# A decoder layer's output projection by seven half-block products over chunk pairs, moved to the end

## The chip, the cores and the metric

One core of one Trainium2 chip runs one launch of the kernel. The metric is device time in microseconds (us). A core has a matmul engine (PE, with its weight loads PEld), a vector engine (DVE), an activation engine (ACT), a third engine for elementwise work (POOL), and SP, which here only issues transfers. Each engine runs its own instructions in order and waits on semaphores for the others. SBUF is the memory on the core, PSUM the banks into which PE accumulates, DRAM the memory off the core.

## What is computed

One layer on 2048 tokens of width 1024, all float32:

- `h = RMSNorm(x) * (1 + scale) + shift`, with shift, scale and gate from a vector `c`
- `P = h @ W_in`, seven groups of 512 columns
- four gMLP groups (`u * mixed(LN(v)) * silu(gate)` in chunks of 128 tokens) and four retention heads (GroupNorm, times `silu(gate)`) give `y`, 2048 x 1024
- `out = x + gate * RMSNorm_post(y @ W_out)`

The change is about the last line's product `y @ W_out`, 2048 x 1024 by 1024 x 1024, and about what is done beside it.

## The kernel before

**Arithmetic.** A float32 operand is split into a high part that PE takes exactly and a low part that is the rest. A block product is three matmuls, high x high, high x low, low x high (`mm3`, `z_mms`), each of 128 rows by up to 512 columns. A high part is a copy on ACT, a low part a subtraction on DVE (`split`, line 170).

**Stages.** The tokens are worked in two halves of 1024, eight chunks of 128 each, two quads of four chunks. A half goes through: retention values (`prv`), queries and keys of two pairs of heads (`pqk`), gMLP values (`pv`), each by `token_unit`, eight slots per chunk; then six *units* (`unit`, line 650), which make the gates and u as seven products of half blocks in place of eight (a scheme of Winograd's kind: blocks A11 to A22 of h and their sums S1 to S4, blocks B11 to B22 of the weights and their sums T1 to T4, three banks X, Y, Z). A unit is 7 products x 4 blocks x 3 = 84 matmuls. Each product's result, after additions out of PSUM on DVE (`then`, `add`), multiplies a tile of y (`used`); in a half's last unit DVE does that for two of the products (`quick`), otherwise POOL does. Then comes the *projection*: `out_unit` per chunk, 16 blocks of w_out x 3 matmuls into two banks, and `out_tail`, which squares (ACT), takes the root (POOL), scales by `gg` (the row gate x g_post), adds x (DVE) and stores. The last chunk of all has its own code (`out_last`).

**What sets the order.** Instructions are issued in the order of the program text on each engine. `Slots` is a clock in that text: a slot is one block (three matmuls), `slots.tick()` moves on, `slots.at(n, fn)` puts `fn`'s instructions n slots later. So each engine has a fixed order, and the engines are tied together only by waits.

**Weights.** `pump` takes the next block of a list (`worder`) and splits it (`wsplit`), and issues transfers for up to three blocks ahead (`wdma`). In the units one product's first slot pumps one block; a half's last unit pumps more (`LAST_PUMPS`). In a unit four weight sums are made by POOL (`combine`). w_out is loaded and split once in each half, 16 blocks, under the last unit and the first `out_unit`.

**Beside the units.** `gate_row` (line 914), started with the first half's second unit, makes `gg`: in four rounds of 33 slots eight additions of 256 columns on DVE over weights that SP loads into three rotating buffers, then a spread over the partitions by two matmuls. `xdiag2` and `xrow` make a row of the second half's 1/rms by matmul, and `hbuild` makes the second half's h, 16 blocks, under the first half's projection, two per chunk; half of them start on POOL and half on DVE.

**Memory.** `slot` takes one of 80 buffers of 2 KB per partition (`big`); all blocks, parts and h live there. y is two tiles per part and half (`yR` for retention, `yT` for gMLP), in pools that are opened and closed as a stack (`opened`, `closed`).

## Time and profile before

| | us |
|---|---|
| median of 3 runs | 895.89 (895.77 to 896.27) |
| the profiled execution | 896.12 |
| its span, first to last instruction | 894.3 |
| PE busy | 865.1 |
| DVE busy | 607.3 |
| POOL busy | 323.8 |
| ACT busy | 294.0 |

The mean granted clock of PE is 0.997 of full. In the rows below a line's number is that of the kernel above; `x240` is a count. In rows of windows the columns are: the stretch, its length, then for PE, PEld, DVE, ACT and POOL the busy time and instructions that began there, the granted clock of PE, the share of the DMA engines and GB/s. A timeline's row may merge several instructions of one kind. What stands in brackets is the idle time of the engine before the instruction and what ended it. PE's matmuls overlap, so their durations are longer than the distance of their starts.

### The profile page before, as it was taken

The page shows a single profiled execution, that of the slowest core. Times are in us where ns is not written, and L with a number is a line of the kernel's source. Part 1 is how long each engine was busy: PE and PEld are TensorE (multiplying, and loading weights), DVE is VectorE, ACT ScalarE, POOL GpSimd, SP SyncE. Part 2 cuts the span into 40 slices and gives each one's busy share as a digit, 9 for nine tenths or more (in the row PEclk, how much of TensorE's full clock was granted, in tenths as well). Part 3 has the DMA queues.
Part 4 walks back from the last instruction along what each step waited for, and adds up shares of the span by engine and source line. Part 5 has one row for each costly group of instructions (what it writes and reads, how often), then busy time and mean ns, then how long its engine had stood idle before and what let it go on. Part 6 is the DMA issues. An engine that isn't in the chain of part 4 may idle for free.

```text
span 894.3 us, 11921 instructions
## 1 busy us (share of the span) xinstructions
PE 865.1 (97%) x4198; PEld 717.4 (80%) x4198; DVE 607.3 (68%) x1217; ACT 294.0 (33%) x585; POOL 323.8 (36%) x399
## 2 busy tenths in 40 slices
PE   2999999999999999899999999999999999999997
PEld 1778888888888878678888888888888888888886
DVE  4989876666997887976676755566499644475332
ACT  4673223233363422533351012012126432352221
POOL 2040353345755654111110033333378554620000
PEclk9999999999999999999999999999999999999999
DMA  8971232210012323744453200110001112142222
GB/s 325 331 246 35 95 107 71 84 35 19 1 48 93 105 94 104 259 153 147 148 177 106 82 1 24 60 36 1 1 1 48 48 57 84 38 143 107 104 94 83
DMA packets 43835, 84.86 MB, mean 95 GB/s; under 512 B 5248, under 2 KB 10496, under 8 KB 43776
## 3 DMA queue, kind: packets, MB, share of 16 engines
q1 hardware_dynamic: 43776, 84.10, 27.6%
q8 instruction: 33, 0.54, 0.3%
q14 instruction: 26, 0.21, 0.1%
HBM read 75.69 MB, written 8.39 MB: 94 GB/s over the span
## 4 chain that ended last, share of the span: by engine, by line
PE 86%; DVE 5%; DMA 4%; issue 3%; ACT 1%; SPq 1%; POOL 0%; DVEq 0%; POOLq 0%; ACTq 0%
PE z L969 6%; PE z L968 6%; PE z L967 6%; PE pqk L210 6%; PE pqk L208 6%; PE pqk L209 6%; PE pv L208 3%; PE pv L210 3%; PE pv L209 3%; PE pY L210 3%; PE pY L209 3%; PE pY L208 3%; PE prv L210 2%; PE prv L209 2%; PE prv L208 2%
## 5 line engine op out<-in xcount | busy, mean ns | idle before, releaser
L208 PE MATMUL pqk<-wh,hh 128*128 128x512 f32 x240 | 102.4, 427 | 0.0
L968 PE MATMUL z<-wl,yh 128*128 128x512 f32 (+1 forms) x264 | 101.1, 383 | 0.2 <-DVE wl L176 0.2
L969 PE MATMUL z<-wh,yl 128*128 128x512 f32 (+1 forms) x264 | 101.1, 383 | 0.0
L967 PE MATMUL z<-wh,yh 128*128 128x512 f32 (+1 forms) x264 | 101.1, 383 | 0.0
L210 PE MATMUL pqk<-wh,hl 128*128 128x512 f32 x240 | 94.5, 394 | 0.0
L209 PE MATMUL pqk<-wl,hh 128*128 128x512 f32 x240 | 93.7, 390 | 0.0
L471 POOL TENSOR_TENSOR rA<-rA,rB 128x512 f32<-128x512 f32 x32 | 42.5, 1327 | 134.8 <-DVE rB L463 100.8
L176 DVE TENSOR_TENSOR wl<-wr,wh 128x512 fp32r<-128x512 f32 x94 | 83.9, 915 | 5.8 <-ACT wh L173 5.8
L485 ACT COPY qkT<-tp 128x512 f32<-128x512 f32 x32 | 18.8, 587 | 172.7 <-PE tp L476 172.7
L579 DVE SCALAR_TENSOR_TENSOR zo<-z,zrs,gg 128x512 f32<-128x512 f32 x30 | 22.4, 745 | 59.2 <-POOL zrs L574 59.2
L173 ACT CAST wh<-wr 128x512 fp32r<-128x512 f32 x96 | 55.5, 619 | 19.9 <-DMA wr<-in_win 7.7
L573 POOL TENSOR_SCALAR zrs<-zss 128x1 f32<-128x1 f32 x15 | 4.5, 300 | 149.0 <-ACT jz L570 149.0
L968 PEld LDWEIGHTS z<-wl,yh 128*128 128x128 f32 x264 | 49.6, 188 | 10.2 <-DVE wl L176 0.5
L969 PEld LDWEIGHTS z<-wh,yl 128*128 128x128 f32 x264 | 49.6, 188 | 10.0 <-DVE yl L559 0.4
L967 PEld LDWEIGHTS z<-wh,yh 128*128 128x128 f32 x264 | 49.6, 188 | 9.8 <-ACT wh L173 0.2
L210 PEld LDWEIGHTS pqk<-wh,hl 128*128 128x128 f32 x240 | 45.0, 188 | 10.4
L637 POOL TENSOR_TENSOR yT<-yT,c 128x512 f32<-128x512 f32 x20 | 30.3, 1516 | 61.3 <-DVE c L658 40.1
L208 PE MATMUL pv<-wh,hh 128*128 128x512 f32 x128 | 52.0, 406 | 0.0
L209 PEld LDWEIGHTS pqk<-wl,hh 128*128 128x128 f32 x240 | 45.5, 189 | 6.6 <-issue 0.2
L208 PEld LDWEIGHTS pqk<-wh,hh 128*128 128x128 f32 x240 | 45.4, 189 | 6.4 <-issue 0.2
L210 PE MATMUL pv<-wh,hl 128*128 128x512 f32 x128 | 50.0, 391 | 0.0
L209 PE MATMUL pv<-wl,hh 128*128 128x512 f32 x128 | 49.9, 390 | 0.0
(233 smaller groups left out, 2215.1 us busy)
## 6 DMA issues: line engine op xcount, KB each, us to landing
wr<-in_win SPq DMA_DIRECT2D x64, 256.0 KB, 3.7
ur<-in_wun SPq DMA_DIRECT2D x48, 256.0 KB, 3.1
slab<-in_wm SPq DMA_DIRECT2D x16, 512.0 KB, 6.4
wr<-in_wout SPq DMA_DIRECT2D x32, 256.0 KB, 4.9
xr<-in_x SPq DMA_DIRECT2D x16, 512.0 KB, 3.2
out<-xr SPq DMA_DIRECT2D x32, 256.0 KB, 2.0
xt<-in_xt SPq DMA_DIRECT2D x24, 256.0 KB, 5.2
xp<-in_x SPq DMA_DIRECT2D x16, 256.0 KB, 2.6
```

The lines of the kernel that those rows point to most:

```text
L173: S.copy(hi, r)
L176: eng.tensor_tensor(lo, r, hi.bitcast(F32), ALU.subtract)
L208: T.matmul(ps, l[0], r[0], start=first, stop=False, skip_group_check=reopened)
L209: T.matmul(ps, l[0], r[1], start=False, stop=False, skip_group_check=reopened)
L210: T.matmul(ps, l[1], r[0], start=False, stop=last, skip_group_check=reopened)
L471: G.tensor_tensor(A, A, box["B"].rearrange("p g h d -> p (g h d)"), ALU.add)
L485: S.copy(qkT, box["tp"])
L579: V.scalar_tensor_tensor(zo, z[c], rs, gg[:, cs], ALU.mult, ALU.mult)
L637: eng.tensor_tensor(y, y, by, ALU.mult)
L967: T.matmul(z, l[0], r[0], start=f, stop=False)
L968: T.matmul(z, l[0], r[1], start=False, stop=False)
L969: T.matmul(z, l[1], r[0], start=False, stop=e)
```

## The change

- The projection of both halves comes after the second half's units. Chunks c and c + 4 of a half are a pair; the pair's y (256 rows) times w_out is done as seven products of half blocks, 84 matmuls per pair, eight pairs, with `pair_sums` (POOL and ACT/DVE) making the sums S1 to S4 and the parts of y, and `out_pair` the additions out of PSUM, squares, gains, roots and results.
- y is written to DRAM by SP (`yspill`: 8 stores of 256 KB, four times) and loaded again per pair (`pair_loads`: four loads of 256 KB).
- w_out is loaded and split once: 28 blocks in the order of the products, with `osplit` making T1 to T4 (POOL two operations and DVE one for T2, POOL one for T4). 14 of them are pumped in the second half's fifth and sixth units (`EXTRA_PUMPS`), 14 in the first pair, one per slot.
- The second half's h is built under the first half's fourth to sixth units (first quad) and under the second half's first four `prv` chunks (second quad).
- `gate_row` starts with the second half's second unit. In the last units POOL does the products into y that DVE did (`quick` is gone).
- `ysplit`, `out_tail`, `z_mms`, `out_unit`, `out_last` are removed.

```diff
-LAST_PUMPS = (0, 0, 1, 1, 1, 1, 2)
+EXTRA_PUMPS = {(0, 5): (0, 0, 0, 1, 0, 1, 1), (1, 4): (0, 1, 0, 1, 0, 1, 1), (1, 5): (0, 1, 1, 1, 1, 2, 2)}
...
+BUILD = {3: ((2, "diag", 0), (9, "row", 0), (14, "x", 0), (15, "x", 1)),
+         4: ((12, "h", 0, 0), (20, "h", 0, 1)),
+         5: ((2, "h", 0, 2), (6, "h", 0, 3), (10, "h", 0, 4), (12, "diag", 1), (14, "h", 0, 5),
+             (17, "row", 1), (18, "h", 0, 6), (22, "h", 0, 7))}
+RV_PUMPS = ((0, 2, 4), (1,), (1,), (1,), (1,), (1,), (1,), (1, 4))
+PAIR = 4 * len(PRODUCTS)
...
+        if kind == "out":
+            raw[i] = {}
+            for key in OUT_RAW[PRODUCTS[n // 4][0]]:
+                t = raw[i][key] = slot("or")
+                SP.dma_start(t, wout[int(key[2]) - 1, 4 * int(key[1]) - 4 + n % 4])
+            return
...
+    kept = {}
+
+    def osplit(i, n, eng, gap):
+        r, (p, kb) = raw.pop(i), divmod(n, 4)
+        what = PRODUCTS[p][0]
+        if what == "T2":
+            t1, t2, t3 = kept["T1", kb], kept["T2", kb], kept["T3", kb] = r["B12"], r["B11"], r["B22"]
+            G.tensor_tensor(t3, t3, t1, ALU.subtract)
+            G.tensor_tensor(t1, t1, t2, ALU.subtract)
+            slots.at(3, lambda: V.tensor_tensor(t2, t3, t2, ALU.add))
+            slots.at(4, lambda: split(i, t2, eng, gap))
+        elif what == "T4":
+            t = r["B21"]
+            G.tensor_tensor(t, t, kept.pop(("T2", kb)), ALU.subtract)
+            slots.at(3, lambda: split(i, t, eng, gap))
+        else:
+            split(i, kept.pop((what, kb)) if what in ("T1", "T3") else r[what], eng, gap)
...
         for i in worder[done[0]:done[0] + ahead]:
-            wdma(i)
+            if i < OUT_BLOCKS or i == worder[done[0]]:
+                wdma(i)
...
+    ydram = ctx.enter_context(tc.tile_pool(name="ydram", bufs=1, space=bass.MemoryType.DRAM))
+    yd = {}
+
+    def yspill(half, part):
+        for ch in range(NCH):
+            t = yd[half, ch, part] = ydram.tile([P, 4, P], F32, name=f"yd{half}{ch}{part}")
+            SP.dma_start(t, (yR, yT)[part][half, ch // QUAD][:, ch % QUAD, :, :])
+
+
+    def pair_loads(half, ch):
+        a = {}
+
+        def load():
+            for m in range(2):
+                for part in range(2):
+                    t = a[f"A{m + 1}{part + 1}"] = slot("ya", (4, P))
+                    SP.dma_start(t, yd[half, ch + QUAD * m, part])
+
+        return a, load
+
+    def pair_sums(a, ops):
+
+        def op(out, x, y, how):
+            def run():
+                if out not in a:
+                    a[out] = slot("ys", (4, P))
+                G.tensor_tensor(a[out], a[x], a[y], how)
+                if out == "S3":
+                    a.pop("A21")
+            return run
+
+        def part(key):
+            def run():
+                hi, lo = ops[key] = slot("yh", (4, P), F32R), slot("yl", (4, P), F32R)
+                src = a[key]
+                S.copy(hi, src)
+                slots.at(0, lambda: V.tensor_tensor(lo, src, hi.bitcast(F32), ALU.subtract))
+            return run
+
+        return ((-8, op("S1", "A21", "A22", ALU.add)), (-6, part("A11")),
+                (-5, op("S2", "S1", "A11", ALU.subtract)), (-2, part("S2")),
+                (0, op("S3", "A11", "A21", ALU.subtract)), (2, part("A12")), (6, part("S3")),
+                (7, op("S4", "A12", "S2", ALU.subtract)), (10, part("S1")), (14, part("A22")),
+                (18, part("S4")))
...
+    def out_pair(begin, half, ch, ops):
+        ps, tmp, xr = {}, {}, []
+        row = [half * HALF + (ch + QUAD * m) * P for m in range(2)]
+        ss = small.tile([P, 2, 2], F32, name="zss", bufs=4)
+        rs = small.tile([P, 2], F32, name="zrs", bufs=4)
+
+        def temp(name, n=1):
+            t = tmp[name] = op.tile([P, 512], F32, name=name, tag="k", bufs=8)
+            return t
+
+        def product(n, bank, first):
+            a = ops.pop(PRODUCTS[n][1])
+            if first:
+                ps[bank] = ps_m.tile([P, 512], F32, name=f"z{bank}", tag="m")
+            for k in range(4):
+                slots.tick()
+                if done[0] < len(worder):
+                    pump(V, 1, 0)
+                mm3(ps[bank], (a[0][:, k, :], a[1][:, k, :]), blocks[OUT_BLOCKS + 4 * n + k],
+                    first and k == 0, k == 3, not first)
...
+        def copy1():
+            S.copy(temp("s1"), ps["X"])
+
+        def add(dst, bank, other):
+            V.tensor_tensor(temp(dst), ps[bank], tmp[other], ALU.add)
...
+        def result(m, n, zg):
+            V.scalar_tensor_tensor(xr[m][:, cols(n)], zg, rs[:, m:m + 1], xr[m][:, cols(n)], ALU.mult,
+                                   ALU.add)
+            SP.dma_start(out[row[m]:row[m] + P, cols(n)], xr[m][:, cols(n)])
...
+        product(0, "X", True)
+        op = begin()
+        for m in range(2):
+            xr.append(op.tile([P, D], F32, name="xr", tag="x", bufs=4))
+            SP.dma_start(xr[m], x[row[m]:row[m] + P, :])
+        after((0, copy1))
+        product(1, "Y", True)
+        after((0, lambda: add("u2", "Y", "s1")))
+        product(2, "X", False)
+        after((0, lambda: square(ps["X"], 0, 0)), (1, lambda: gain(temp("g11"), ps["X"], 0)))
+        product(3, "Y", False)
+        after((0, lambda: add("u3", "Y", "s1")))
+        product(4, "Z", True)
+        after((0, lambda: add("c22", "Z", "u3")), (1, lambda: square(tmp["c22"], 1, 1)),
+              (2, lambda: gain(tmp["c22"], tmp["c22"], 1)))
+        product(5, "Y", False)
+        after((0, lambda: add("c21", "Y", "s1")), (1, lambda: square(tmp["c21"], 1, 0)),
+              (2, lambda: gain(tmp["c21"], tmp["c21"], 0)), (3, lambda: root(1)),
+              (6, lambda: result(1, 0, tmp["c21"])), (7, lambda: result(1, 1, tmp["c22"])))
+        product(6, "Z", False)
+        after((0, lambda: add("c12", "Z", "u2")), (1, lambda: square(tmp["c12"], 0, 1)),
+              (2, lambda: gain(tmp["c12"], tmp["c12"], 1)), (3, lambda: root(0)),
+              (6, lambda: result(0, 0, tmp["g11"])), (7, lambda: result(0, 1, tmp["c12"])))
...
-            slots.at(1, lambda: times(V if quick else G, g))
+            slots.at(1, lambda: times(G, g))
...
-                if k in (0,) or (un == len(UNITS) - 1 and k in (1, 2, 3)[:LAST_PUMPS[n]]):
+                if k <= EXTRA_PUMPS.get((half, un), (0,) * 7)[n]:
...
+    def build1(q, kb):
+        n = q * KB + kb
+        hbuild(1, q, kb, hb["x"].pop(0), hb[q], kb % 2 == 1, (3, 5), True)
+        if n + 2 < 2 * KB:
+            fetch1(n + 2)
...
+            if half == 1 and ch == 0:
+                for n in range(KB):
+                    slots.at(6 + 3 * n, partial(build1, 1, n))
+                slots.at(4, partial(yspill, 0, 1))
+            ps = token_unit(half, 0, ch, "prv", () if half == 0 else RV_PUMPS[ch])
...
-            if un == 1 and half == 0:
+            if un == 1 and half == 1:
...
+            if un == 2:
+                slots.at(4, partial(yspill, half, 0))
+            if half == 0 and un in BUILD:
+                for t, what, *args in BUILD[un]:
+                    slots.at(t, partial({"diag": diag1, "row": row1, "x": fetch1, "h": build1}[what],
+                                        *args))
+            if half == 1 and un == len(UNITS) - 1:
+                pairs = [(h, c, {}, *pair_loads(h, c)) for h in range(2) for c in range(QUAD)]
+                slots.at(10, pairs[0][4])
+                for t, fn in pair_sums(pairs[0][3], pairs[0][2]):
+                    slots.at(PAIR + t, fn)
             unit(half, un, up)
-        op = None
-
-        def close():
-            closed()
-            return opened(f"out{half}")
-
-        for pos in range(NCH):
-            if half == 0:
-                for i in range(2):
-                    n = 2 * pos + i
-
-                    def build(n=n):
-                        q, kb = divmod(n, KB)
-                        hbuild(1, q, kb, hb["x"].pop(0), hb[q], kb % 2 == 1, (3, 5))
-                        if n + 2 < 2 * KB:
-                            hb["x"].append(xdma(1, *divmod(n + 2, KB)))
-
-                    slots.at(8 * i + 4, build)
-            op = out_unit(op, half, pos, close)
-    closed(3)
+
+    slots.at(3, partial(yspill, 1, 1))
+    pools = []
+
+    def begin():
+        if not pools:
+            closed(3)
+            pools.append(opened("out"))
+        return pools[0]
+
+    for n, (h, c, ops, a, load) in enumerate(pairs):
+        if n + 1 < len(pairs):
+            slots.at(PAIR - 20, pairs[n + 1][4])
+            for t, fn in pair_sums(pairs[n + 1][3], pairs[n + 1][2]):
+                slots.at(PAIR + t, fn)
+        out_pair(begin, h, c, ops)
+    slots.flush()
+    closed()
```

## Rows read from the trace of the kernel before

**Rows 1.** the page: busy us, share, instructions; the chain by engine
```profile
PE 865.1 (97%) x4198; PEld 717.4 (80%) x4198; DVE 607.3 (68%) x1217; ACT 294.0 (33%) x585; POOL 323.8 (36%) x399
...
PE 86%; DVE 5%; DMA 4%; issue 3%; ACT 1%; SPq 1%; POOL 0%; DVEq 0%; POOLq 0%; ACTq 0%
```

**Rows 2.** windows by unit and projection: us, busy (x instructions), PEclk, DMA, GB/s
```profile
249.18:270.03 20.85, 20.85 (x101) 17.56 (x100) 17.96 (x37) 11.88 (x24) 11.65 (x11) 1.00 0.10 38
...
289.31:308.51 19.20, 19.20 (x85) 15.69 (x84) 15.81 (x23) 7.13 (x13) 12.18 (x9) 1.00 0.35 112
...
327.79:351.49 23.70, 21.48 (x87) 17.10 (x86) 16.75 (x22) 6.48 (x12) 11.29 (x9) 0.93 0.28 89
351.49:375.39 23.90, 21.53 (x91) 16.59 (x90) 23.22 (x49) 10.03 (x18) 9.49 (x7) 1.00 0.65 233
375.39:463.28 87.89, 87.66 (x385) 71.92 (x384) 62.61 (x94) 34.94 (x74) 15.48 (x22) 1.00 0.46 160
...
684.91:705.76 20.85, 20.85 (x101) 17.55 (x100) 17.95 (x37) 11.88 (x24) 11.63 (x11) 1.00 0.27 87
...
743.84:762.88 19.04, 19.04 (x85) 15.77 (x84) 8.69 (x13) 5.22 (x10) 10.02 (x9) 1.00 0.18 56
...
781.92:800.96 19.04, 19.04 (x85) 15.77 (x84) 14.31 (x21) 9.95 (x19) 7.30 (x6) 1.00 0.50 166
800.96:888.48 87.52, 87.51 (x409) 73.27 (x407) 36.79 (x57) 21.68 (x54) 6.36 (x15) 1.00 0.26 94
```

**Rows 3.** timeline of PE at the gate row: start, us, what, idle before
```profile
332.13 0.40 PE L209 MATMUL pY<-sl,wh 128*128 128x512 f32 x1
332.36 0.40 PE L210 MATMUL pY<-sh,wl 128*128 128x512 f32 x1
334.39 0.38 PE L942 MATMUL gps<-ah,ones 128*128 128x256 f32 x1 [1.63 <-ACT ah L936]
...
336.97 0.63 PE L210 MATMUL pX<-hh,wl 128*128 128x512 f32 x1
337.39 0.63 PE L208 MATMUL pX<-hh,wh 128*128 128x512 f32 x1
```

**Rows 4.** windows: the stretch behind that stall
```profile
336.30:340.60 4.30, 4.30 (x13) 3.40 (x12) 2.65 (x5) 0.00 (x0) 0.00 (x0) 0.60 0.95 330
```

**Rows 5.** timeline of DVE: start us, us, what
```profile
330.71 1.77 DVE L176 TENSOR_TENSOR wl<-ur,wh 128x512 fp32r<-128x512 f32 x1
...
380.10 3.69 DVE L176 TENSOR_TENSOR wl<-wr,wh 128x512 fp32r<-128x512 f32 x6
```

**Rows 6.** timeline of POOL: start us, us, what
```profile
330.27 1.67 POOL L637 TENSOR_TENSOR yT<-yT,c 128x512 f32<-128x512 f32 x1 [0.97 <-DVE c L658]
...
785.55 1.28 POOL L193 TENSOR_TENSOR ut<-ur 128x512 f32<-128x512 f32 x1
```

**Rows 7.** tile gg: count, ns min/median/max, first and last start
```profile
L929 DVE SCALAR_TENSOR_TENSOR gg<-wgt,sc,gg x28: 473/916/1589, 274.4 to 358.8; 128x256 f32<-128x256 f32 x28
```

**Rows 8.** groups by line and shape: xcount | busy us, mean ns
```profile
L658 DVE TENSOR_TENSOR c<-pZ,u 128x512 f32<-128x512 f32 x24 | 16.5, 686 | 19.1 <-PE pZ L210 19.0
...
L570 ACT ACTIVATE jz<-z 128x512 bf16<-128x512 f32 x30 | 17.8, 595 | 60.0 <-PE z L969 60.0
...
L301 POOL TENSOR_TENSOR xt<-xt,rb 128x512 f32<-128x512 f32 x12 | 16.8, 1412 | 2.6 <-ACT rb L280 2.6
...
L637 POOL TENSOR_TENSOR yT<-yT,c 128x512 f32<-128x512 f32 x20 | 30.3, 1516 | 61.3 <-DVE c L658 40.1 <-ACT c L645 21.2
...
L254 DVE TENSOR_SCALAR dgr<-cst_t,rsh 128x128 fp32r<-128x128 f32 x8 | 2.2, 279 | 0.0
```

**Rows 9.** timeline of DVE at the end of the kernel
```profile
890.00 1.42 DVE L1026 SCALAR_TENSOR_TENSOR xr<-zg,zrs,xr 128x512 f32<-128x512 f32 x2 [0.55 <-POOL zrs L1023]
```

**Rows 10.** the page's DMA issues: xcount, KB each, median us to landing
```profile
out<-xr SPq DMA_DIRECT2D x32, 256.0 KB, 2.0
```

**Rows 11.** timeline of SP's DMA issues in the sixth unit
```profile
359.66 1.37 SPq L168 DMA_DIRECT2D wr<-in_wout  x3
```

## Prediction: what the change does to the time

> **What bounds the kernel now.** I read the page's busy line and chain first: TensorE (PE) is busy 97% of the span and owns 86% of the chain that ended last [rows 1]. So a change pays by taking columns from PE and costs by making it wait. The windows by stage come next [rows 2]. A unit in which nothing is late is 84 matmuls of 512 columns in 19.04 us, 0.2267 us each. The second half's six units take 684.91 to 800.96, 116.05 us; the first half's take 249.18 to 375.39, 126.21 us, with the same matmuls. The 10.16 us between them are the gate row, the next half's builds and what these make PE wait for: its fifth and sixth units take 23.70 and 23.90 us. The timeline of PE there [rows 3] shows it standing at 332.36 until the gate row's cast is there (1.63 us), and soon after its matmuls start 0.42 to 0.43 us apart, where 0.23 is usual. The granted clock is 0.60 in that stretch [rows 4], so most of it ran at 1.2 instead of 2.4 GHz: eight matmuls, some 1.6 us lost behind one stall. Behind the stall is DVE. An operation of two SBUF operands takes it 0.605 us in a row of six [rows 5] and 1.77 us at 330.71, where POOL was busy from 330.27 for 1.67 us [rows 6]; POOL's own is 1.28 us where DVE leaves it alone [rows 6]. The gate row's additions take 0.47 us at least and 0.92 in the median [rows 7]. The two engines' SBUF work adds up where both are busy.
>
> **Projection.** Before, 375.39 to 463.28 and 800.96 to 888.48 [rows 2], 87.89 + 87.52 = 175.4 us for 768 matmuls' worth of columns. After, 8 pairs x 7 products x 4 blocks x 3 = 672, at 0.2267 us 152.3 us. Shapes and order within a product stay, so I carry the rate over. **-23.1 us.**
>
> **First half's units.** The gate row leaves them, and so does the build's place in the sixth: 126.21 falls towards 116.05, **-10.2**. The builds now lie under units 4 to 6, with four spread matmuls, **+0.9**. The gate row comes to the second half with eight 256-column matmuls, about 0.12 us each by the half of 0.2267, **+1.0**. What the moved work makes PE wait is counted below.
>
> **End.** Before, the last 256-column part goes through square, root and two results; DVE's two results start at 890.00 and take 1.42 us [rows 9]. After, the last product first needs DVE's addition out of PSUM (0.69), then a square of 512 columns (0.60, where 256 columns were) [rows 8]; DVE has two results of the partner chunk and a gain to pass meanwhile, and four stores end together instead of two. I count 0.7 for the addition and 1.0 for the rest, from 0.2 (all beside it) to 2.5. **+1.7.**
>
> So far -29.7 us (23.1 + 10.2 - 0.9 - 1.0 - 1.7, rounded terms). Everything else is waiting.
>
> **How much SBUF work DVE and POOL have.** I count operations, POOL's at 1.29 us, DVE's of two SBUF operands at 0.605, gate-row ones at 0.47 [rows 5 to 7], and compare with 19.04 us. The scale is the first half's third unit (289.31 to 308.51) [rows 2]: nine POOL operations (11.6), seven low parts (4.2), ten gate-row operations (4.5) are 20.3 us in 19.2 without a PE stall to speak of, so 0.945 of the sum fits; PE's wait starts where DVE is more than about 2.7 us late, since an addition out of PSUM is emitted four slots before PE reopens the bank (4 x 3 x 0.2267).
>
> - Second half, unit 5: POOL 10 (six weight sums, four products into y), 12.9; DVE 11 low parts and the gate row, 6.7 + 4.5. Sum 24.1, times 0.945 is 22.8: 3.7 over.
> - Unit 6: POOL 13, of which eight are the T2 sums of w_out and two the first pair's S1 and S2, 16.8; DVE 16 low parts, four T2 additions, two parts of y, the rest of the gate row, 16.0. Sum 32.8, 31.0: 12.0 over. DVE stands in order behind its T2 additions, which wait for POOL, and the low part of A11 and the additions of c21 and c12 are queued behind them; PE waits for those.
> - First pair: POOL 9 (S3, S4, the last product into y, four T4 sums, the next pair's S1, S2), 11.6; DVE 14 low parts of weights, seven of y, two gains, 13.9. Sum 25.5, 24.1: 5.1 over.
> - Later pairs: POOL 4, 5.2; DVE seven low parts, three gains, four results of 0.71 [rows 9], 8.9. Sum 14.1, 13.3 of 19.04: 5.7 us free, where the backlog drains.
>
> Over in all 20.8, less 5.7 drained in the second pair, less the 2.7 of lead: 12.4 us of PE waits, and one stretch at the low clock, 1.6 [rows 3, 4]. **+14.0.** From below, what the gate row cost where it stood: unit 5 of the first half, 23.70 - 19.04 = 4.7. From above, no lead, no drain, the full sums: 25.3 and three low-clock stretches, 30.
>
> Within this lies the first pair's spill. Its scratch tiles lie where y's second part was (the pools are closed and opened at the same base), so the copy of X out of PSUM can wait for four stores of y, and these for POOL's last product (1.52 us [rows 8], on DVE before). Four stores, about 0.45 us apart and 2.0 us to land [rows 10, 11], end some 8 us into the pair; product three needs the copy at 5.4. Alone 2.7 us; beside DVE's backlog it runs in the same time, so I add nothing (to 5 if POOL is late as well). On ACT the weight casts stand behind this copy, on SP the pair's x loads, four raw blocks and the next pair's loads behind the stores. The two spills of the first half wait in SP ahead of loads wanted much later: 0, up to 1 if POOL holds y back.
>
> **First half's last unit.** POOL eight (three of them builds, 1.41 [rows 8], counted at 1.29), 10.3; DVE 11 low parts, nine operations of builds (six at 0.71, three at 0.605), eight diagonals of 0.28 [rows 8], 15.0. Sum 25.3, 23.9: 4.9 over, less 2.7: **+2.2**. The eight later builds under the next half's first 21.8 us hold about 22 by the same count, so little drains and little is added; 0 to 7. Where the builds stood, under the first projection, POOL had nothing else to add; that cover is gone.
>
> The Trainium skill speaks against the change here: "SBUF — State Buffer", section "Who interferes with whom", says that a DVE instruction with two SBUF inputs and a GpSimd one that reads SBUF exclude each other for the whole instruction. The pair 330.71 and 330.27 agrees [rows 5, 6], while 20.3 us of such work in 19.2 says that it is not quite whole. By the rule alone the factor would be 1; that is the third rival.
>
> **Sum.** -29.7 + 14.0 + 2.2 = -13.5 on the profiled execution, 896.12 (span 894.3 and 1.8 outside it), which stands 0.2 above the median of 895.89: 882.6, said as 883.
>
> **Rivals.**
> - *POOL runs ahead.* It isn't tied to PE: T2 sums can start when their weights land, and POOL is idle nearly half of a second-half unit (10.0 of 19.04, [rows 2]). Then only the gate row's old stall (4.7) and the spill (2.7) are left: -29.7 + 7.4 = 873.8. Against: unit 6's weights need slots that PE has just freed, and SP is held by the gate row's tiles.
> - *Every pair is late once.* DVE has ten operations in a pair's first eight slots, 6.5 us, and S3 and S4 (2.6) block some: 9.1 against the 8.2 until product four needs u2. 0.9 us in each of seven pairs, +6.5: 889.5. For it: results wait for the root on POOL. Against: DVE is 5 us short of full in a pair.
> - *Slower: DVE and POOL take turns in full.* Place: units 5 and 6 of the second half, first pair, and the first half's last unit. Sums at factor 1, no lead, no drain: 5.1 + 13.8 + 6.5 and 6.3, with three low-clock stretches (4.8), 36.5: -29.7 + 36.5 = +6.8, 903. It decides from 29.7 us of waits. For it 330.71; against, the third unit's 20.3 in 19.2, and the first half's sixth, which waited under 4 us with DVE busy 23.22 of 23.90 [rows 2].
>
> **How the numbers follow.** Forecast 0.52 (its own range 877 to 890), POOL ahead 0.24 (868 to 879), every pair late 0.12 (886 to 894), in turns 0.08, something else 0.04. Range 870 to 896: below it some of POOL ahead, above it the slower case. This kernel's measurement tells some 0.2%, 1.8 us, from no change. Faster: 0.52 + 0.24 + 0.11 and a little of the rest, 0.88; within 0.2%: 0.04; slower: 0.08.
>
> **What would show it.** The seven later pairs at 19.04 us each (152.3 in all but for the first) show the columns; each 1 us more there speaks for the second rival. The first half's units near 117 show that the gate row left; its sixth at 21.5 shows the builds' price. PE standing on DVE's low part of y, or on c22's addition, in unit 6 and the first pair, with POOL busy throughout, shows the backlog; ACT's copy of X waiting for a DMA shows the spill. A second half with clean units and a first pair near 22 us would show POOL ahead. What makes it wrong: PE waits far from 16 us in all, or a rate of the pairs other than 0.2267 us a matmul.

## The result, and the profile after

The changed kernel takes 939.0 us against 896.1 of the kernel before, run beside it: a ratio of 1.0466 (95% interval 1.0436 to 1.0496), slower by 4.7%. One of its four executions ran at a granted clock of 0.56 and took 1454.8 us; the ratio goes by the other three, 935.5 to 939.5. The prediction was 883, with 870 to 896 as its range. The profiled execution took 938.51 us, 936.7 of them span. The matmuls that the change takes away are gone, and PE stands still instead. The busy line of the page of after, to be read beside [rows 1]:

```profile
PE 860.2 (92%) x4078; PEld 703.0 (75%) x4078; DVE 678.8 (72%) x1266; ACT 318.0 (34%) x621; POOL 409.2 (44%) x446
```

PE has 120 instructions fewer and is busy only 5 us less. Windows by stage show where the time went and where the granted clock fell, with columns as in [rows 2]: the first half's six units and the stage behind them, the second half's third, fifth and sixth unit, the first pair, and the other seven pairs with the last matmuls:

```profile
249.20:371.62 122.42, 118.44 (x525) 96.78 (x524) 82.65 (x131) 53.67 (x95) 68.93 (x51) 1.00 0.32 97
371.62:419.60 47.98, 46.00 (x193) 36.58 (x192) 42.92 (x66) 14.58 (x23) 9.05 (x6) 0.96 0.47 154
...
638.10:661.80 23.70, 21.22 (x85) 16.73 (x84) 14.65 (x23) 7.24 (x14) 12.57 (x10) 0.93 0.53 181
...
681.18:706.14 24.96, 21.73 (x87) 17.01 (x86) 20.27 (x23) 8.27 (x16) 15.28 (x11) 0.93 0.25 79
706.14:745.00 38.86, 24.62 (x87) 18.65 (x86) 26.04 (x31) 11.66 (x22) 18.73 (x13) 0.82 0.53 183
745.00:788.34 43.34, 24.03 (x85) 18.30 (x84) 28.82 (x38) 13.89 (x29) 15.46 (x11) 0.80 0.46 170
788.34:928.90 140.56, 135.94 (x589) 109.41 (x587) 107.13 (x140) 48.01 (x110) 62.09 (x56) 1.00 0.40 143
```

Without any wait the prediction's own sum is 896.12 - 29.7 = 866.4 us, so 938.51 holds 72 us of waits and low clock, where 16.2 (14.0 + 2.2) were predicted. By stage, against 19.04 us a unit or pair (the 1.0 for the gate row's matmuls is inside the second half's losses here):

| stage | measured | unhindered | lost | predicted lost |
|---|---|---|---|---|
| first half, six units | 122.4 | 116.9 | 5.5 | 2.2 |
| stage behind them | 48.0 | 43.5 (before) | 4.5 | little |
| second half, units 1 to 4 | 83.3 | 78.0 | 5.3 | 0 |
| units 5, 6 and first pair | 107.2 | 57.1 | 50.0 | 14.0 |
| seven later pairs | 140.4 | 133.3 | 7.1 | 0 (6.5 in a rival) |
| behind the last matmul | 7.9 | 5.8 (before), 7.5 by the forecast | 0.4 | 0 |

So one term failed above all: units 5 and 6 and the first pair. PE's timeline there (start, us, what, idle before and what ended it) has four stops of 5.8 us and more, behind each of which matmuls start 0.43 us apart instead of 0.23, and a shorter one:

```profile
728.46 0.79 PE L239 MATMUL pY<-hh,wh 128*128 128x512 f32 x1 [6.13 <-DVE u L772]
729.06 0.63 PE L240 MATMUL pY<-hl,wh 128*128 128x512 f32 x1
729.48 0.63 PE L241 MATMUL pY<-hh,wl 128*128 128x512 f32 x1
...
740.63 0.79 PE L239 MATMUL pZ<-sh,wh 128*128 128x512 f32 x1 [6.75 <-DVE c L772]
...
751.58 0.50 PE L241 MATMUL zY<-wh,yl 128*128 128x512 f32 x1 [2.75 <-DVE yl L619]
...
759.92 0.79 PE L239 MATMUL zX<-wh,yh 128*128 128x512 f32 x1 [5.78 <-ACT s L654]
...
781.02 0.77 PE L239 MATMUL zY<-wh,yh 128*128 128x512 f32 x1 [10.59 <-DVE u L657]
```

What is DVE doing when PE waits for it at 728.46? Windows over the same place (the length; busy PE, PEld, DVE, ACT and POOL; granted clock, DMA share, GB/s):

```profile
718.00:731.00 13.00, 6.87 (x26) 5.29 (x25) 2.58 (x4) 1.24 (x2) 4.30 (x4) 0.84 0.98 342
...
730.00:734.00 4.00, 3.88 (x10) 2.55 (x8) 2.20 (x2) 0.36 (x1) 3.84 (x4) 0.54 0.92 333
...
738.00:742.00 4.00, 1.37 (x3) 1.16 (x4) 4.00 (x5) 1.94 (x4) 2.77 (x2) 0.50 0.00 0
```

From 718 to 731 DVE works 2.58 of 13 us and POOL 4.30, while the DMA engines are busy 98% of the time. That is not a backlog of DVE and POOL, as I had forecast; they wait for loads. At 738 it is one: DVE is busy without a gap. Both regimes stand within 20 us of each other. The timelines of DVE, POOL, SP and ACT give the order of events:

```profile
721.67 0.68 DVE L751 TENSOR_TENSOR yT<-yT,pX 128x512 f32<-128x512 f32 x1
727.11 0.69 DVE L203 TENSOR_TENSOR or<-or 128x512 f32<-128x512 f32 x1 [4.76 <-DMA or<-in_wout]
727.72 0.68 DVE L772 TENSOR_TENSOR u<-pY,s 128x512 f32<-128x512 f32 x1
731.80 1.75 DVE L203 TENSOR_TENSOR or<-or 128x512 f32<-128x512 f32 x1 [3.40 <-DMA or<-in_wout]
...
724.48 1.26 POOL L201 TENSOR_TENSOR or<-or 128x512 f32<-128x512 f32 x1 [12.79 <-DMA or<-in_wout]
725.82 1.26 POOL L202 TENSOR_TENSOR or<-or 128x512 f32<-128x512 f32 x1
...
701.52 5.07 SPq L1037 DMA_DIRECT2D wgt<-in_wg  x3
...
716.40 1.37 SPq L176 DMA_DIRECT2D or<-in_wout  x3
717.81 2.91 SPq L599 DMA_DIRECT2D ya<-yd  x4
720.85 9.86 SPq L176 DMA_DIRECT2D or<-in_wout  x13
749.33 7.10 SPq L589 DMA_DIRECT2D yd<-yT  x8
...
763.59 4.94 SPq L176 DMA_DIRECT2D or<-in_wout  x6
...
759.28 0.58 ACT L654 COPY s<-zX 128x512 f32<-128x512 f32 x1 [11.49 <-DMA yd<-yT]
...
771.59 2.18 ACT L184 CAST wh<-or 128x512 fp32r<-128x512 f32 x4 [6.01 <-DMA or<-in_wout]
```

SP asks for the gate row's tiles (L1037) in order between its other loads, and each waits until DVE has freed one of three tiles. So the raw blocks that T2 needs (L176) are asked for from 716.40 on, sixteen within 15 us and four blocks of y among them. POOL waits 12.79 us for the first, and DVE's addition of T2 (L203) waits for POOL: the row names a DMA, but L203 overwrites a tile that POOL's L202 reads, and it starts at 727.11, where L202 ends at 727.08. The addition u3 that PE needs (u2, u3, c21, c22 and c12 are the additions out of PSUM), ready to run, stands in DVE's order behind L203. In the pair ACT's copy of X waits for the spill (11.49 us), six raw blocks are asked for behind spill, x rows and next loads, and ACT, DVE's low parts and the addition u3 wait for them: the 10.59 us.

### The profile page after: what moved, and what is told of

Same layout as the page of the kernel before. It is cut to its first block, busy times and chain, and to the rows that moved or that the text cites. A ratio compares the mean times of both kernels' runs of the same rounds, so it can differ in the third digit from the quotient of the medians.

```text
span 936.7 us, 11918 instructions
## 1 busy us (share of the span) xinstructions
PE 860.2 (92%) x4078; PEld 703.0 (75%) x4078; DVE 678.8 (72%) x1266; ACT 318.0 (34%) x621; POOL 409.2 (44%) x446
## 5 line engine op out<-in xcount | busy, mean ns | idle before, releaser
L187 DVE TENSOR_TENSOR wl<-wr,wh 128x512 fp32r<-128x512 f32 x62 | 65.0, 1062 | 0.2
L239 PE MATMUL zY<-wh,yh 128*128 128x512 f32 x96 | 38.8, 404 | 15.1 <-DVE u L657 13.9
L493 DVE TENSOR_TENSOR rA<-pqk,cos_t 128x512 f32<-128x512 f32 x28 | 19.3, 688 | 39.3 <-PE pqk L241 39.3
L184 ACT CAST wh<-ut 128x512 fp32r<-128x512 f32 x48 | 28.5, 620 | 52.0 <-POOL ut L224 51.9
L239 PE MATMUL pZ<-sh,wh 128*128 128x512 f32 x96 | 38.3, 399 | 6.8 <-DVE c L772 6.8
L609 POOL TENSOR_TENSOR ys<-ya 128x512 f32<-128x512 f32 x16 | 21.9, 1371 | 48.1 <-DMA ya<-yd 32.6
L187 DVE TENSOR_TENSOR wl<-ut,wh 128x512 fp32r<-128x512 f32 x48 | 40.0, 853 | 2.6 <-ACT wh L184 2.6
L561 DVE TENSOR_SCALAR yq<-o,gmv,grs 128x128 f32<-128x128 f32 x64 | 23.3, 405 | 25.4 <-POOL grs L554 25.4
L241 PE MATMUL zY<-wh,yl 128*128 128x512 f32 x96 | 38.2, 398 | 2.7 <-DVE yl L619 2.7
L440 ACT ACTIVATE vh<-pv,nbv,rsv 128x128 f32<-128x128 f32 x64 | 24.1, 457 | 47.4 <-POOL nbv L435 47.4
```

Of the source, the lines that this page charges most:

```text
L184: S.copy(hi, r)
L187: eng.tensor_tensor(lo, r, hi.bitcast(F32), ALU.subtract)
L239: T.matmul(ps, l[0], r[0], start=first, stop=False, skip_group_check=reopened)
L241: T.matmul(ps, l[1], r[0], start=False, stop=last, skip_group_check=reopened)
L440: S.activation(vh[:, g, :], ps[:, g * P:(g + 1) * P], AF.Identity, bias=nb[:, g:g + 1], scale=rs[:, g:g + 1])
L493: V.tensor_tensor(A, ps.rearrange("p (g d) -> p g d", g=8), tab["cos"][:, ch, :].unsqueeze(1).broadcast_to([P, 8, 64]), ALU.mult)
```

## Experiments: what makes PE wait

I held two theories. *Late transfers*: loads asked for late on SP, and queues kept in order, so that a ready operation stands behind a waiting one. *Port sums*, the prediction's: DVE's and POOL's SBUF work adds up to more than the stretch holds. Times of single runs are read against 938.5; the three executions that the ratio goes by lie 4 us apart, so I read these runs by the times of their stages.

**1. The gate row elsewhere.** Three runs. Back in the first half's second unit (`if un == 1 and half == 0:`):

> The changed kernel, with the gate row put back into the first half's second unit; the operations are the same. Theory A (late transfers: in the second half SP stands in order behind the gate row's rotating tiles, so the raw blocks of w_out leave late, POOL's T2 sums and ACT's casts wait for them, and the additions that PE needs stand behind these in DVE's order): the sixth unit of the second half falls from 38.9 us to 27 or less and the fifth from 25.0 to about 20; the first half's units grow from 122.4 to about 130, since gate row and builds meet there. Total about 920 us. Theory B (port sums: DVE and POOL have too much two-operand SBUF work there, as the prediction had it): only the gate row's own 7 us of port time leave, the sixth unit stays above 33, total 935 or more.

Half of it in each half's units (`gate_row(up, (2 * half, 2 * half + 1))`):

> The changed kernel with two rounds of the gate row in the first half's second and third units and two in the second half's, so that it meets neither the builds' last units nor the pumping of w_out. Theory A: the second half's sixth unit 27 us or less as with the gate row back in the first half, the fifth about 20, and the first half's units near 124; total 912 to 920. Theory B: the port time of the gate row alone leaves the fifth and sixth units, 4 to 7 us; total 931 or more.

In the second half's stage of q and k products:

```
-            if un == 1 and half == 1:
-                gate_row(up)
...
             early = half == 0 and pr_ == 0
+            if half == 1 and pr_ == 0:
+                gate_row(rp)
```

> The gate row goes from the second half's units to that half's earlier stage of q and k products, where SP has only loads to ask for and no unit waits. Late transfers: the sixth unit no longer has SP behind gate-row tiles, so the last weight blocks land earlier; units 1 to 5 at 19.0 to 19.4 each, the sixth 25 to 30 (38.9 before the edit), first pair 38 to 43, the time 920 to 928. Port sums: the gate row's 9 us of DVE work leave unit 5 and 6, so the same fall of unit 5 (25.0 to 19), the sixth to about 27, and the q and k stage longer by less than 1 us. The two part only if the stage of q and k grows (POOL idle there: it must not by port sums).

930.17 (e1), 923.10 (e4) and 918.64 us (e5). In e5 the second half's units 2 to 5 take 19.04 each, the sixth 28.45 (38.86 before the edit), the first pair still 43.77, and the stage of q and k grows by 2.8. So the gate row cost 5.3 us in units 1 to 4, 5.9 in the fifth and 10.4 in the sixth where the change puts it. Back in the first half it costs 12.8 there (135.2 for its six units). The sixth unit takes 28.07 in e1 and 28.80 in e4: just short of what late transfers said (27 or less) and far from port sums (above 33 in e1; 4 to 7 us off units 5 and 6 in e4, where 16.0 left). The times lie between the two theories, e4's nearer to late transfers. In e5 PE's stop for u3 is gone and POOL's wait for the first raw block of T2 is 3.92 instead of 12.79 us, so the gate row did hold these loads; the stop for c22 stays:

```profile
704.05 1.42 POOL L201 TENSOR_TENSOR or<-or 128x512 f32<-128x512 f32 x1 [3.92 <-DMA or<-in_wout]
...
720.22 0.80 PE L239 MATMUL pZ<-sh,wh 128*128 128x512 f32 x1 [6.96 <-DVE c L772]
```

For e5's units I had given both theories nearly the same numbers, and its growth of 2.8 does not part them either, as I had meant it to: 1.0 of it is the gate row's own eight matmuls, and the one new stop of PE, 1.58 us, is for an operation that stands in DVE's order behind one of the gate row's (L1067), which took 1.34 us beside POOL and 0.42 in e6 with POOL idle.

**2. Loads and spill of the first pair.** The eight raw blocks left are asked for ahead of the spill:

```
+    slots.at(0, lambda: [wdma(i) for i in worder[done[0]:]])
     slots.at(3, partial(yspill, 1, 1))
```

> The changed kernel, with the eight raw blocks of w_out that the first pair pumps (for T4 and B22) asked for on SP ahead of the y spill, the x rows and the next pair's loads instead of behind them; same operations on every other engine in the same order. Theory A: PE's wait of 10.6 us for the addition of u3 in the first pair goes with ACT's 6.0 us wait for these raw blocks; first pair from 43.3 us to 29 to 33, total 925 to 929. Theory B: the port sums are the same, so the first pair stays at 40 or more and the total at 936 to 939.

And, with that, the first pair's scratch over the half of y that was spilled earlier, x rows 15 slots later (`temp("s1")` ahead of the x tiles, `slots.at(15, x_loads)`):

> As the kernel with the raw blocks first, and the first pair's scratch tiles laid over the half of y that was spilled long before (its x rows, asked for 15 slots later, lie over the part spilled last). Theory A: ACT no longer waits 11.5 us for the stores of y, PE's 5.8 us wait for the copy of X goes; first pair 22 to 26 us, total 917 to 922. Theory B, or the rival that DVE's backlog fills the time anyway: first pair stays within 3 us of the kernel with the raw blocks first.

930.58 (e2) and 927.39 us (e3). PE's row of e2 where the wait of 10.59 was:

```profile
773.58 0.47 PE L239 MATMUL zY<-wh,yh 128*128 128x512 f32 x1 [1.80 <-DVE u L657]
```

The wait for u fell to 1.80 and the one for ACT's copy grew to 9.70, as the spill now stands behind more loads; the pair went from 43.34 to 36.52. Both the pair and the time lie between the two expectations. With the scratch moved that wait went too, and one of 5.46 us for u3 came behind it: 32.22, again between the two. DVE's and POOL's work is the same in all three kernels, so 11 us of the pair were transfers: their order on SP and the stores that the copy waited for. The sixth unit did not move (38.86).

**3. Order within DVE's queue.** T2's addition and split five slots later (`slots.at(8, ...)`, `slots.at(9, ...)` for 3 and 4):

> T2's addition and its split are put five slots later in DVE's and ACT's order; the work of every engine is the same. Late transfers with in-order queues: the additions u3 and c22 no longer stand behind T2's addition, which waits for a late block; the sixth unit falls from 38.9 by 8 to 13 us, the first pair may grow by 2 to 5, the time falls by 5 to 10 to 929 to 934. Port sums: only order changes, so unit and pair together (82.2) stay within 3 us, time 936 to 941.

938.30 us (e6): the sixth unit fell by 9.1 to 29.79, as late transfers said, and the first pair grew by 8.7 to 52.05, so that the two together stayed at 81.8 (82.2), as port sums said. PE no longer waits for c22, but then for the pair's first y block:

```profile
736.47 0.80 PE L239 MATMUL zX<-wh,yh 128*128 128x512 f32 x1 [6.63 <-ACT yh L618]
```

The forecast of port sums came true here, but not by its mechanism. Ahead of this stop's end DVE stands idle for 6.67 us and POOL's sums take their unhindered 1.26; the cast of that y block stands in ACT's order behind two weight casts that waited 12.53 us for raw blocks:

```profile
734.65 1.24 ACT L184 CAST wh<-or 128x512 fp32r<-128x512 f32 x2 [12.53 <-DMA or<-in_wout]
735.80 0.61 ACT L618 CAST yh<-ya 128x512 fp32r<-128x512 f32 x1
...
735.30 1.62 DVE L187 TENSOR_TENSOR wl<-or,wh 128x512 fp32r<-128x512 f32 x1 [6.67 <-ACT wh L184]
```

So the queue order only named the place of the wait, and what fed it was late loads. The partner chunk's results three slots later (`(9, ... result(0, 0, ...)), (10, ... result(0, 1, ...))` for 6 and 7):

> The partner chunk's results move from slots 6 and 7 of a pair to 9 and 10. If each pair is late once because the addition u2 stands behind two results in DVE's order, the seven later pairs fall from 140.4 to 133 to 135 us (19.04 each) and the time by 5 to 7, to 931 to 934. If POOL and DVE in turns make them late, the pairs stay at 139 to 141.

932.07 us (e7), and the seven later pairs are 19.04 each. DVE and PE of the changed kernel (two results and a low part, then u2, with PE waiting), and below it e7's window of the seven pairs, in which PE is busy from end to end:

```profile
833.16 1.77 DVE L671 SCALAR_TENSOR_TENSOR xr<-g,zrs,xr 128x512 f32<-128x512 f32 x1
834.86 0.74 DVE L671 SCALAR_TENSOR_TENSOR xr<-c,zrs,xr 128x512 f32<-128x512 f32 x1
835.52 0.68 DVE L619 TENSOR_TENSOR yl<-ys,yh 128x512 fp32r<-128x512 f32 x1
836.12 0.68 DVE L657 TENSOR_TENSOR u<-zY,s 128x512 f32<-128x512 f32 x1
...
836.95 0.47 PE L239 MATMUL zY<-wh,yh 128*128 128x512 f32 x1 [1.09 <-DVE u L657]
```

```profile
788.80:922.09 133.29, 133.29 (x589) 110.21 (x588) 107.76 (x139) 48.35 (x110) 63.09 (x56) 1.00 0.45 150
```

**4. The first half.** Spread rows at slots 20 and 26 instead of 9 and 17, three more low parts in its last unit, one in each of the eight chunks of the stage behind:

> First half only: the spread rows go to slots 20 and 26, three more low parts are pumped in the last unit, and the following stage takes one low part in each slot. By order within DVE's queue: the first half's units fall from 122.4 to 117 to 119, the following stage from 48.0 to 44 to 45, the time by 5 to 9, to 930 to 934. By port sums: the same work in the same 160 us, so only what the stage after takes in is gained, 1 to 3 us, 936 to 938.

935.78 us (e8). The units took 123.2 and the stage behind 45.3, together 168.5 where 170.4 were: 1.9 less, as port sums said. Six kernels of this document with the same code in these stages (the changed one, e2, e3, e5, e6, e7) took 169.5 to 172.2, so only 1.0 of it lies outside their spread. A fall by 5 to 9 is excluded, so the order that I changed is not what makes these stages late; that the work itself is too much is the reading left, and not shown.

**5. All of it, and what is left.** All edits of 1 (the third), 2, 3 and 4; the same without T2's later addition; and that with raw blocks asked for two splits ahead (`i <= worder[done[0]] + 1`), each run several times beside the kernel before:

> All edits together: gate row in the second half's q and k stage, raw blocks of w_out asked for ahead of the spill, first pair's scratch over the half of y that was spilled earlier, partner results at slots 9 and 10, the first half's builds and pumps moved, and T2's addition five slots later. By late transfers and queues in order nearly all waits go: second half's units 116 to 122, first pair 24 to 30, later pairs 133.3, the time 882 to 891, under before's 896. By port sums the work is all still there: the sixth unit and the first pair keep 20 to 30 us of waits together, the time 898 to 908.

> The same, with T2's addition where the change had it (slot 3). By queues in order the sixth unit keeps its wait for c22 (some 7 us, and low clock after it): sixth unit 27 to 29, first pair 29 to 33, the time 6 to 10 above the one with T2 late. By port sums the two are within 3 us of each other.

> As the one before (T2's addition at slot 3), but the raw blocks of w_out are asked for two pumps ahead instead of one, so that T2's sums on POOL find them landed. By late transfers the wait of POOL for them (3.9 and 3.3 us) and of the sixth unit for c22 (7 us) fall to 2 or less, so the sixth unit is 20 to 24 and the time is 5 to 9 below the one before. By port sums no more than 2 us. If the ring of slots is what holds the loads, asking earlier gains nothing either.

903.21 us (e9; ratio 1.0073, 1.0053 to 1.0092), 901.75 (e10; 1.0061, 1.0046 to 1.0076) and 899.78 (e11; 1.0045, 1.0031 to 1.0059). The sixth unit and the first pair together take 61.0, 61.9 and 59.2 us, and the first has its waits in the pair (19.96 + 41.03), the second in both (27.88 + 34.05). Order and late loads are mended as far as these edits go, and 21 us stay over 38.1. Here port sums forecast better on all three times: waits of 20 to 30 us kept, no more than 3 us between e9 and e10, no more than 2 from asking earlier. In e11's first pair DVE is busy 31.70 of 33.34 us; in its sixth unit it is not (20.24 of 25.84), and PE stands there 4.08 us for c22 behind a T2 addition that waits, so not all of the 21 is full engines. To part POOL's sums from loads I left out of e11 the eight weight sums of T1 and T3 on POOL and kept the loads; then, with the sums in, loaded B12 and B22 early, into the part of y spilled by then, made the four T3 sums in the fifth unit and put the first pair's scratch into the 80 buffers:

> Leaves out the eight weight sums on POOL for the T1 and T3 blocks of w_out; the loads, DVE's additions and all matmuls stay, at the same places. If late loads are what is left, the sixth unit and the first pair stay at 54 to 60 together (59.2 before the edit). If it is POOL's sums and DVE in turns with them, some 12 us of POOL, they fall to 42 to 48, and the time to 883 to 889.

```
+    def early_load(kb):
+        for q, key in ((0, "B12"), (1, "B22")):
+            t = yR[1, q][:, kb, :, :].rearrange("p h t -> p (h t)")
+            kept["T1" if q == 0 else "T3", kb] = t
+            SP.dma_start(t, wout[int(key[2]) - 1, 4 * int(key[1]) - 4 + kb])
```

> The raw blocks B12 and B22 of w_out are loaded two units earlier into the part of y that is spilled by then, T2 takes the raw block of B11 that is there already, and the T3 sums run on POOL in the fifth unit; four T1 sums stay late. Late loads: sixth unit and first pair fall from 59.2 to 40 to 46, the time to 880 to 888. Port sums: half of the sums are moved to a unit that POOL and DVE fill less, so a fall of 5 to 8 only, and up to 1 us more in the fifth unit, 891 to 895.

893.06 us (e14, one run) and 897.30 (e12; ratio 1.0022, 1.0010 to 1.0034): unit and pair 53.2 and 56.7. Without the sums 6.0 of the 21 go, which is just beyond what late loads said (54 to 60) and at most half of what port sums did (a fall of 11 to 17); early loads and sums give 2.5, less than both. In e14's first pair it is DVE that is full, 30.98 of 32.80 us, though those sums are gone:

```profile
716.70:749.50 32.80, 24.47 (x85) 18.57 (x86) 30.98 (x39) 16.59 (x33) 17.70 (x10) 0.84 0.66 225
```

Then the first half's builds spread four and four over its fifth and sixth unit, T1's sums early too, and low parts of the first pair put behind the additions:

```
-                if done[0] < len(worder):
+                if done[0] < len(worder) and (n > 1 or k % 2 == 0):
                     pump(V, 1, 0)
```

> As the one with early raw blocks, but the first half's eight builds are spread over its fifth and sixth units, four and four, and the stage after has its old pumps. Port sums: DVE's and POOL's work in the sixth unit falls by two builds of 3.6 us, so that unit falls from 26.5 to 20 to 22 and the fifth grows by at most 1: the time 4 to 6 below e12's. By order in DVE's queue about the same fall; this run tells size, not cause.

> As e13, with the four T1 sums moved too: the raw blocks of B11 are loaded in the fourth unit, T3's sums run on POOL in the fourth and T1's in the fifth. If DVE's and POOL's work in turns is what is left, 4 sums of 1.7 us leave the stretch in which DVE is full: sixth unit and first pair fall from 57.8 to 50 to 53, the time to 890 to 893. If transfers are what is left, no fall beyond 2 us.

> As e15, with weight blocks split in every other slot of the first pair's first two products, so that four low parts stand behind the additions u2 and u3 in DVE's order instead of ahead of them. With DVE full the additions come 2 to 5 us earlier and the low parts have slack until the later products: first pair falls by 2 to 5 more, the time to 886 to 891. If transfers are what is left, nothing changes, or the last blocks are late and it grows by 1 to 2.

896.95 us (e13; 1.0019, 1.0010 to 1.0028), 894.72 (e15; 0.9994, 0.9984 to 1.0003) and 893.83 (e16; 0.9978, 0.9969 to 0.9987). e13's last unit of the first half fell to 22.0 as expected and the fifth grew by 2.0, not 1; the gain of 2.3 in the units and the stage behind them is mostly lost again later, and the time is 0.4 below e12's where 4 to 6 were expected. e15's unit and pair take 54.2 (57.8 in e13), between the two expectations, and e16's pair 33.99 (34.78), a smaller fall than expected; both times are above their expectations (890 to 893, 886 to 891). e16 is faster than the kernel before, though by 0.2% only. Its windows: fifth and sixth unit, first pair, other pairs, and three stretches inside the first pair:

```profile
676.80:697.40 20.60, 19.68 (x86) 15.51 (x85) 16.29 (x14) 7.72 (x14) 20.52 (x14) 1.00 0.08 25
697.40:716.80 19.40, 19.32 (x85) 15.69 (x84) 18.60 (x23) 11.05 (x21) 10.63 (x7) 1.00 0.33 109
716.80:750.80 34.00, 24.69 (x86) 18.76 (x85) 32.15 (x37) 13.96 (x30) 16.55 (x11) 0.85 0.61 217
750.80:884.06 133.26, 133.26 (x589) 110.20 (x587) 109.37 (x140) 48.56 (x111) 63.29 (x56) 1.00 0.45 150
...
720.80:724.80 4.00, 1.27 (x4) 0.86 (x4) 4.00 (x4) 2.53 (x6) 2.35 (x2) 0.88 0.57 195
728.80:732.80 4.00, 1.82 (x9) 1.16 (x7) 4.00 (x4) 0.00 (x0) 4.00 (x3) 1.00 1.00 349
732.80:736.80 4.00, 2.13 (x5) 1.78 (x6) 4.00 (x5) 0.51 (x2) 2.24 (x2) 0.66 1.05 400
```

While PE waits DVE is busy without a gap, and its operations and POOL's take some 1.7 us each where both run:

```profile
728.30 6.74 POOL L205 TENSOR_TENSOR or<-or 128x512 f32<-128x512 f32 x4
...
730.51 1.75 DVE L631 TENSOR_TENSOR yl<-ys,yh 128x512 fp32r<-128x512 f32 x1
732.18 1.74 DVE L187 TENSOR_TENSOR wl<-yR,wh 128x512 fp32r<-128x512 f32 x1
733.84 0.68 DVE L672 TENSOR_TENSOR u<-zY,s 128x512 f32<-128x512 f32 x1
```

## Why the prediction was wrong, step by step

- **Columns: right.** Later pairs that nothing hinders take 19.04 us, 133.29 for seven. The -23.1 is there.
- **First half: right in kind.** The gate row left (units 2, 3 and 5 at 19.04), but the price of the builds, 2.2 in the last unit and "little" after it, was 5.5 and 4.5. Another order did not bring it back (e8); the cause is not shown beyond that.
- **End: right.** 7.9 us behind the last matmul against 5.8, 2.1 longer, forecast 1.7.
- **The step that failed: "Over in all 20.8, less 5.7 drained in the second pair, less the 2.7 of lead: 12.4 us of PE waits, and one stretch at the low clock, 1.6. +14.0."** It measured 50.0 us. The step took all waiting in units 5 and 6 and the first pair for one queue of work, and cost three things at nothing or too little. First, the gate row's place in SP's and DVE's order: moved to where the raw blocks of w_out are asked for, it held their loads until 716.40, and e5, which only moves it to an earlier stage, shortens units 5 and 6 by 16.3. My sum had its work on DVE there at 7.2 (4.5 and 2.7); how the 16.3 divide between that work and the held loads is not shown. In units 1 to 4 I gave it no price beyond its matmuls; it cost 5.3, as it had in the first half. So most of the -10.2 was no gain: the same waits came back later in the kernel. Second, the spill ("it runs in the same time, so I add nothing"): raw blocks behind it and the copy that waited for it cost 11 us (e2, e3). The spill did not run beside a backlog of DVE: DVE was busy 28.82 of the pair's 43.34 us. Third, the low clock: I allowed one stretch, and each of the four long stops was followed by one.
- **What of port sums holds.** With those mended, 21 us stay in e11 in the sixth unit and the first pair, and e16, with eight sums moved ahead of the sixth unit, still loses 16.9 in units 5, 6 and pair, low clock included. That is the size of the +14.0 by luck: the +14.0 had the gate row and all eight sums in it, where e16 has no gate row and four of the sums, and 15.0 of the 16.9 lie in the pair, where my count was 5.1 over. The pair's count was short: 14 + 7 + 2 operations of DVE, where e16's pair has 37 (20 low parts of weights, eight of y, three gains, six additions out of PSUM, which I counted nowhere). At 0.605 us [rows 5] these are 22.4 us by estimate, more than 19.04 before POOL comes in, and the rest of DVE's 32.15, some 9.8, is what they are stretched. The Trainium skill, "SBUF — State Buffer", section "Who interferes with whom", calls the port pair that DVE shares with GpSimd an exclusive lock, and has a DVE instruction with two SBUF inputs contend with a GpSimd one that reads SBUF. The trace agrees nearly: beside each other both take some 1.7 us an operation (POOL's four in 6.74, above), where 0.605 and 1.28 [rows 5, 6] one after the other are 1.89.
- **The rival "every pair is late once": true as well**, not instead: 7.1 us against its 6.5 (seven times 0.9 is 6.3), by the mechanism named there (e7). I should have added it to the sum, since it excluded nothing.
- **The slower rival** had the right sign, mostly for the wrong reason: waits above 29.7, but of the 50.0 in its main place 16.3 went with the gate row, held loads among it, and 11 with the first pair's transfers, and of the 21 left not all is DVE and POOL in turns.

Not settled: how the last 15 us of e16's first pair divide between DVE's own operations, POOL beside them and the low clock. DVE is full there, which is shown; the 22.4 and 9.8 above are an estimate, and no run took DVE's low parts away, or all of POOL's work.

## What to carry to other kernels

When work is moved, follow each of its DMAs and each of its additions into the in-order queue that it enters, and ask what stands ready behind it there; a sum of engine time says nothing about that. A wait that a reorder removes is gained only if the work that fed it also comes sooner (e6 moved 9 us from one stage to the next). Mechanisms that can be at work together are terms of one sum, not rivals.

## What the runs showed of the hardware

- DVE and POOL beside each other: DVE's 0.68 us (0.605 from start to start in a row) becomes 1.74 to 1.78, POOL's 1.26 becomes 1.70 to 1.75, in the first half's last unit as in the first pair.
- Behind PE's stops of 5.8 to 10.6 us the next 7 to 12 matmuls start 0.43 us apart, at the lower of the two clocks (granted clock 0.50 to 0.54 in such windows). A stop of 2.75 us left the clock at full speed: the rows after 751.58 start 0.23 apart. The length of a stop alone does not decide it: behind one of 2.74 us in e11 (below) and one of 1.63 in the kernel before [rows 3] matmuls also start 0.42 to 0.43 apart.

```profile
729.39 0.79 PE L241 MATMUL zY<-wh,yl 128*128 128x512 f32 x1 [2.74 <-DVE yl L619]
729.98 0.63 PE L239 MATMUL zY<-wh,yh 128*128 128x512 f32 x1
730.41 0.63 PE L240 MATMUL zY<-wl,yh 128*128 128x512 f32 x1
```

- Seventeen transfers of 256 KB asked for within 13 us kept the DMA engines at 98% and 342 GB/s.
